# One hybrid decoder layer: a scan constant in PSUM, carries read from the scan buffers, fused operations, and GLA queries decayed in one pass

## The chip, the cores and the metric

The kernel runs on one core of a Trainium2 chip. The metric is the device time of one execution in microseconds (us). The five engines named below are TensorE (PE in the profile; PEld are its weight loads), VectorE (DVE), ScalarE (ACT), GpSimd (POOL) and SyncE (SP, which here only issues transfers). They run side by side, each in its own fixed order, and wait for each other through semaphores. SBUF is the on-chip memory of 128 partitions; PSUM is the smaller memory of eight banks into which TensorE writes.

## The reference

One decoder layer on 2048 positions of width 1024, in float32: three token mixers on the same normalised input, one output projection with residual, and a gated FFN with residual.

```python
h = rms_norm(x, norm_mix_g)
gq, gk, gv, g_lr, g_gate, sq, sk, sv, hq, hf, hi, h_gate = split(h @ w_in)
# A) GLA, 4 heads of 48 / 96, and C) HGRN2, 4 heads of 128 / 64: gated linear recurrences
#    S_t = diag(exp(log_f_t)) S_{t-1} + k_t^T v_t ;  o_t = q_t S_t
o_a = rms_norm(gla(gq, gk, gv, log_alpha)) * silu(g_gate)
o_c = rms_norm(gla(hq, 1 - f, hi, log_f)) * silu(h_gate)
# B) stick-breaking attention, 6 heads of 64, strictly causal:
z = q_b @ k_b.T * 64 ** -0.5
A[t, s] = sigmoid(z[t, s]) * prod_{s < j < t} (1 - sigmoid(z[t, j]))
o_b = rms_norm(A @ v)
x = x + concat(o_a, o_b, o_c) @ w_out
gate, up = split(rms_norm(x) @ w_ffn_up)
return x + (silu(gate) * up) @ w_ffn_down          # d_ff = 2816
```

## The kernel before, in words

Matrix products run in TensorE's fp32r format with each operand split into a high part and the rest (`split`, `conv_w`: ACT makes the high part, DVE or POOL the rest), three matmuls per product: high·high, high·low, low·high. The two FFN products are also split into seven block products of half size, numbered 1 to 7, whose operands are sums and differences of blocks (`sub`, `add`).

The work goes through stages. *Input projections* come first. Then the *mixers* run together. Attention is cut into units of one head, one group of 512 queries and one block of 512 keys, and each unit into four steps of 128 queries. `z_step` computes z on TensorE, two sigmoids on ACT (`kp` for 1 − sigmoid, `w` for sigmoid), a running product of `kp` from the last key to the first on DVE (L993, `tensor_tensor_scan`, whose second operand is not used: `op1` is bypass), and the product `w` · `pr` on POOL, or on DVE for some steps (L997). The last value of the running product is the carry into the next key block: POOL copies it into a column of its own (`ca`, L996). `t_step` transposes `w`, five steps behind, and `a_step` multiplies it with the values, seven steps behind. The two recurrences work on chunks of 128 positions (`hg_chunk`, `gla_chunk`) in levels of doubling block size (`decay_levels`): at each level queries and keys are multiplied by decays (DVE L1071 and L1112, POOL L1117 and L1106), the decays by each other (POOL L1121), TensorE forms the scores (`sch`, `scg`), and a copy by mask (DVE L1075) takes them out of PSUM. GLA's two heads share a partition range, so that its queries lie in two copies that see the same decays. The recurrences' score tiles take turns in a ring of three PSUM banks (`c_pss`).

TensorE's order in the mixers is fixed by the program's order (`Chain`); the other engines are ordered by a scheduler that follows a simulated timeline. Attention's end overlaps the *output projection* (`Out`): `load` fetches a tile of 128 positions and normalises its heads (14 squares on ACT with their sums, DVE multiplies, POOL gates), `turn` transposes it, three matmuls per block multiply it, `norm` and `left` prepare the FFN's input, which `left_sums` stores in DRAM as `xs_s`.

*FFN up* goes over two halves of the positions and 22 blocks of columns, the seven products in the order 1, 5, 6, 2, 3, 7, 4; `left_in` loads and converts the left operands (`ah`, `al`). *FFN down* runs the seven products in the order 1, 2, 5, 6, 3, 7, 4, each over 11 steps k with eight PSUM banks. `left_dn` and `right_dn` load (`ar`, `br`, chains `xa`, `xb`), combine and convert each step's operands (`dah`, `dal`, `dbh`, `dbl`); `flush_dn` adds a finished product to the accumulators `acc`, which start from the residual, and stores finished quarters to `out`. All these transfers are issued by SP, one after the other. Every tile takes its buffer from a pool with a number of buffers (`bufs`), and a new tile waits until the last use of the one before in its buffer.

Of the kernel before, what the change touches and what calls it, by code (L numbers as in the profile page):

```python
# [19 lines left out]
P = 128  # L20
# [42 lines left out]
def hybrid_block(ctx: ExitStack, tc: tile.TileContext, x, norm_mix_g, w_in, gla_w_decay,  # L63
# [740 lines left out]
    class Out:  # L804
        def open(self):
# [5 lines left out]
            self.pt = open_pool(self.st, "d_pt", 1, PSUM, side="right")  # L811

        def load(self, t):
# [15 lines left out]
            dve.tensor_scalar(ms[:, 4:14], ms[:, 4:14], 1.0 / SD, EPS, op0=ALU.mult,  # L829
                              op1=ALU.add)  # L830
            rs = rsqrt_newton(self.sm, ms, 14, "rm")
            for a, b, w, i, j in segs:
                mv = m[:, a:b].rearrange("p (h d) -> p h d", d=w)
# [3 lines left out]
            pool.tensor_tensor(m[:, 768:], m[:, 768:], gt[:, 384:], op=ALU.mult)  # L837
            mv = m[:, 384:768].rearrange("p (h d) -> p h d", d=SD)
            pool.tensor_tensor(mv, mv, gs64.unsqueeze(1).to_broadcast([P, SH, SD]), op=ALU.mult)
# [4 lines left out]
        def turn(self, prep, hf):  # L844
            t, m, _, mh, ml = prep
            pt = self.pt.tile([P, 4, P], F32, tag="pt", name=f"mt{t}_{hf}")
# [15 lines left out]
        def left(self, t, xt, kh):  # L862

            pt = self.pt.tile([P, KH, P], F32, tag="pt", name=f"xt{t}_{kh}")
# [61 lines left out]
    with ExitStack() as ph:  # L926
# [11 lines left out]
        ps_s = open_pool(prc, "c_pss", 3, PSUM)  # L938
# [20 lines left out]
        def z_step(u, b):  # L959
            h, g, c = u.h, u.g, u.c  # L960
            if b == 0:
                if u.diag:
                    u.q = sio.tile([P, 2, 512], F32, tag="sq", name=f"sq{h}_{g}", bufs=3)
                    for s in range(2):
# [3 lines left out]
                    u.carry = [sbk.tile([P, 1], F32, tag=f"ca{i}", name=f"ca{h}_{g}_{i}", bufs=4)  # L968
                               for i in range(4)]
                else:  # L970
                    p = units[u.i - 2]
                    u.q, u.carry = p.q, p.carry
# [12 lines left out]
            if u.diag:  # L985
# [3 lines left out]
            pr = sbk.tile([P, 513], F32, tag="pr", name=f"pr{h}_{g}_{c}_{b}")  # L989
            act.activation(kp[:, :n], z, AF.Sigmoid, scale=-1.0)  # L990
            act.activation(w, z, AF.Sigmoid)  # L991
            kr = kp[:, n::-1] if n < 512 else kp[:, ::-1]
# [4 lines left out]
            (dve if (b in DVE_B0 if g == 0 else b == DVE_B) else pool).tensor_tensor(w, w, pr[:, 1:n + 1], op=ALU.mult)  # L997
            u.ws.append(w)

        def t_step(u, s):  # L1000
# [5 lines left out]
            wh = sbw.tile([P, 512], F32, tag="wth", name="wth" + nm, bufs=8)[:, t0:]  # L1006
# [43 lines left out]
        def decay_levels(nm, nq, nk, q, k, f, st, score, block, hold, eng, qeng):  # L1050
# [9 lines left out]
            def tv(ap, s, h, rep):  # L1060

                m = ap.shape[2] // 2
                v = ap.rearrange("p n (b s) -> p n b s", s=2)[:, :, :, s]
                return v.unsqueeze(3).to_broadcast([P, nk, m, h])
# [529 lines left out]
```

## Time and profile before

| | |
|---|---|
| median of 3 runs (lowest, highest) | 3147.08 us (3138.09, 3147.41) |
| profiled execution | 3147.62 us, its span 3145.8 us |
| TensorE busy, weight loads | 2831.5 us (90%), 2309.9 us |
| VectorE, ScalarE, GpSimd busy | 2116.2 (67%), 1344.4 (43%), 1639.2 us (52%) |
| transfers | 389.82 MB, mean 124 GB/s |

The page divides the span into 40 slices. Each digit is the busy share of a slice in tenths, and PEclk is the clock granted to TensorE, in tenths of full speed:

```profile
PE   5898999997888889878888799999999997899998
DVE  8886665886888888988866455555755553267443
PEclk9999999998889998989988899999999998999999
```

### The profile page before, as it was taken

Reading aid. Unit: us, or ns where it says so; the run is one execution under the profiler, and the core shown is the slowest. Engines: PE = TensorE matmul, PEld = TensorE weight load, DVE = VectorE, ACT = ScalarE, POOL = GpSimd, SP = SyncE. Lnnn points to the kernel's source line nnn. Section 1 sums busy time; section 2 is a strip of 40 time slices with the busy share of each in tenths; the row PEclk is TensorE's granted clock in tenths of the full one; section 3 lists DMA queues with packets and bytes.
Section 4 is the critical chain, followed back from the end, with each engine's and each line's share of the span. In section 5 each row is a group of like instructions: output and inputs, shape, how many; then the busy total and the mean of one; then the engine's idle time right before and its main releaser. Section 6 shows DMA issues by size and latency. Waiting matters only on the chain. (4 is left out here: it accounts for less than half of the span.)

```text
span 3145.8 us, 43879 instructions
## 1 busy us (share of the span) xinstructions
PE 2831.5 (90%) x14882; PEld 2309.9 (73%) x14882; DVE 2116.2 (67%) x3508; ACT 1344.4 (43%) x2834; POOL 1639.2 (52%) x1640
## 2 busy tenths in 40 slices
PE   5898999997888889878888799999999997899998
PEld 5897878996666666655666588888788885677776
DVE  8886665886888888988866455555755553267443
ACT  5554534453555555566644333333433332323222
POOL 5342554344787887854633244444544442257635
PEclk9999999998889998989988899999999998999999
DMA  3534432536533333123354332222422225564173
GB/s 116 159 108 134 139 127 97 136 94 166 153 104 107 98 100 93 58 94 108 130 173 161 134 114 85 87 87 84 142 87 81 81 81 216 212 234 144 64 241 131
DMA packets 346095, 389.82 MB, mean 124 GB/s; under 512 B 59152, under 2 KB 258064, under 8 KB 344080
## 3 DMA queue, kind: packets, MB, share of 16 engines
q1 hardware_dynamic: 341776, 381.77, 38.4%
q0 software_dynamic: 4096, 5.25, 0.5%
q8 instruction: 119, 1.95, 0.3%
q14 instruction: 104, 0.85, 0.1%
HBM read 278.93 MB, written 108.00 MB: 123 GB/s over the span
## 5 line engine op out<-in xcount | busy, mean ns | idle before, releaser
L1390 PE MATMUL gu<-ah,uh 128*128 128x512 f32 x1232 | 481.3, 391 | 10.1 <-ACT ah L248 10.1
L1391 PE MATMUL gu<-al,uh 128*128 128x512 f32 x1232 | 481.8, 391 | 6.0 <-DVE al L249 5.9
L1392 PE MATMUL gu<-ah,ul 128*128 128x512 f32 x1232 | 481.0, 390 | 0.0
L249 POOL TENSOR_TENSOR ul<-bs,uh 128x512 fp32r<-128x512 f32 x176 | 241.6, 1374 | 243.2 <-ACT uh L248 243.2
L249 POOL TENSOR_TENSOR ul<-us,uh 128x512 fp32r<-128x512 f32 x132 | 176.6, 1339 | 203.6 <-ACT uh L248 203.6
L1390 PEld LDWEIGHTS gu<-ah,uh 128*128 128x128 f32 x1232 | 232.3, 189 | 60.3 <-ACT ah L248 12.0
L1391 PEld LDWEIGHTS gu<-al,uh 128*128 128x128 f32 x1232 | 232.5, 189 | 56.9 <-DVE al L249 8.7
L1552 PE MATMUL dn<-dbh,dah 128*128 128x512 f32 x616 | 224.6, 402 | 48.4 <-ACT dbh L248 41.8
L1392 PEld LDWEIGHTS gu<-ah,ul 128*128 128x128 f32 x1232 | 232.3, 189 | 48.1
L245 DVE TENSOR_TENSOR h<-h,gu 128x512 f32<-128x512 f32 x176 | 120.9, 687 | 205.3 <-PE gu L1392 123.5
L1553 PE MATMUL dn<-dbl,dah 128*128 128x512 f32 x616 | 243.9, 396 | 12.7 <-POOL dbl L249 12.6
L1554 PE MATMUL dn<-dbh,dal 128*128 128x512 f32 x616 | 242.4, 395 | 3.1 <-DVE dal L249 3.0
L248 ACT ACTIVATE uh<-bs 128x512 fp32r<-128x512 f32 x176 | 110.9, 632 | 299.8 <-PE gu L1391 299.6
L993 DVE TENSOR_TENSOR_SCAN pr<-kp,ca 128x513 f32<-128x513 f32 x144 | 213.2, 1484 | 22.0 <-ACT kp L990 17.7
L997 POOL TENSOR_TENSOR w<-w,pr 128x512 f32<-128x512 f32 (+1 forms) x174 | 191.8, 1102 | 46.0 <-DVE pr L993 26.0
L990 ACT ACTIVATE kp<-z 128x512 f32<-128x512 f32 (+1 forms) x240 | 128.0, 533 | 183.4 <-PE z L104 168.7
L104 PE MATMUL z<-sk,sq 128*128 128x512 f32 (+1 forms) x480 | 170.7, 440 | 14.5 <-ACT w L991 8.1
L107 PE MATMUL wt<-ident,w 128*128 128x128 f32 x816 | 147.9, 294 | 39.2 <-POOL w L997 34.3
L1552 PEld LDWEIGHTS dn<-dbh,dah 128*128 128x128 f32 x616 | 118.4, 194 | 80.5 <-ACT dbh L248 49.3
L249 DVE TENSOR_TENSOR dal<-ar,dah 128x1024 fp32r<-128x1024 f32 x44 | 65.0, 1485 | 163.1 <-ACT dah L248 163.0
L248 ACT ACTIVATE uh<-us 128x512 fp32r<-128x512 f32 x132 | 83.1, 631 | 193.0 <-PE gu L1391 130.6
L104 PEld LDWEIGHTS z<-sk,sq 128*128 128x128 f32 x480 | 80.7, 208 | 104.7 <-issue 37.9
(385 smaller groups left out, 7845.1 us busy)
## 6 DMA issues: line engine op xcount, KB each, us to landing
us<-in_w_ffn_up SPq DMA_DIRECT2D x88, 512.0 KB, 3.8
ar<-hs_s SPq DMA_DIRECT2D x88, 512.0 KB, 4.0
hs_s<-h SPq DMA_DIRECT2D x44, 512.0 KB, 2.6
br<-in_w_ffn_down SPq DMA_DIRECT2D x88, 256.0 KB, 3.2
sk<-sk_s SPq DMA_DIRECT2D x60, 256.0 KB, 2.9
st<-xs_s SPq DMA_DIRECT2D x14, 1024.0 KB, 5.2
xt<-in_x SPq DMA_DIRECT2D x24, 512.0 KB, 4.8
sq<-sq_s SPq DMA_DIRECT2D x48, 256.0 KB, 4.8
```

The source lines that it names most:

```text
L104: self._add(nc.tensor.matmul(*a, **k))
L107: self._add(nc.tensor.transpose(*a, **k))
L248: act.activation(wh, st, AF.Copy)
L249: eng.tensor_tensor(wl, st, wh.bitcast(F32), op=ALU.subtract)
L993: dve.tensor_tensor_scan(pr[:, n::-1], kr, kr, 1.0 if u.diag else u.carry[b], op0=ALU.mult, op1=ALU.bypass)
L997: (dve if (b in DVE_B0 if g == 0 else b == DVE_B) else pool).tensor_tensor(w, w, pr[:, 1:n + 1], op=ALU.mult)
L1390: pe.matmul(pv, bh[:, k, :], ah[:, :, k, :], start=(k == 0), stop=False)
L1391: pe.matmul(pv, bh[:, k, :], al[:, :, k, :], start=False, stop=False)
L1392: pe.matmul(pv, bl[:, k, :], ah[:, :, k, :], start=False, stop=(k == KH - 1))
L1552: pe.matmul(pss[i], ah[:, ts_], bh, start=(k == 0), stop=False)
L1553: pe.matmul(pss[i], ah[:, ts_], bl, start=False, stop=False)
L1554: pe.matmul(pss[i], al[:, ts_], bh, start=False, stop=(k == NK - 1))
```

## The change

*Mixers.* The scan's unused operand becomes a column of ones in a PSUM bank of its own (`c_ps1`), for as long as the recurrences run; the score ring `c_pss` has two banks instead of three. The 47 scans that come after the recurrences keep the old operand. Two scan buffers with shifted views (`at`) hold the carries, so that the next scan reads the last column of an earlier one and the copies to `ca` go. GLA's decays `ga` are loaded twice, and a level multiplies both copies of the queries by one instruction. The states' decay and sum become one fused DVE instruction for each head or pair (`scalar_tensor_tensor`), 60 + 30 of them, in place of 30 products on POOL and 30 sums on DVE.

*Output projection.* A tile's 14 squares on ACT become one, with three sums on DVE; normalising and gating become 14 fused DVE instructions in place of three DVE and three POOL products. Three more PSUM banks (`d_px`) hold transposes once the mixers are through.

*FFN up.* The first `ah`, `al` buffers are taken in the reverse order of the products, which changes whose space the first one reuses.

*FFN down.* The order becomes 1, 5, 6, 2, 3, 7, 4; loads keep the program's order; `br` has three buffers; products 5 and 7 are added to both accumulators from PSUM on DVE (before, ACT copied them and POOL added the copy); half of product 6's adds are put off, two for each step of the next product.

```diff
+            sq = self.wk.tile([P, D], F32, tag="sq", name=f"msq{t}", bufs=1)
+            act.activation(sq, m, AF.Square)
             for a, b, w, i, j in segs:
-                for h in range(j - i):
-                    sj = self.sm.tile([P, GDV], BF16, tag="sj", name=f"sj{t}_{i}_{h}", bufs=1)
-                    act.activation(sj[:, :w], m[:, a + h * w:a + (h + 1) * w], AF.Square,
-                                   accum_out=ms[:, i + h:i + h + 1])
+                dve.tensor_reduce(ms[:, i:j], sq[:, a:b].rearrange("p (h d) -> p h d", d=w),
+                                  axis=AX.X, op=ALU.add)
...
-                dve.tensor_tensor(mv, mv, rs[:, i:j].unsqueeze(2).to_broadcast([P, j - i, w]),
-                                  op=ALU.mult)
-            pool.tensor_tensor(m[:, 0:384], m[:, 0:384], gt[:, 0:384], op=ALU.mult)
...
+                    dve.scalar_tensor_tensor(m[:, cs], m[:, cs], rs[:, n:n + 1], g_,
+                                             op0=ALU.mult, op1=ALU.mult)
...
-        ps_s = open_pool(prc, "c_pss", 3, PSUM)
+        ps_s = open_pool(prc, "c_pss", 2, PSUM)
+        ps_1 = open_pool(prc, "c_ps1", 1, PSUM)
+        ones = [ps_1.tile([P, 512], F32, name="one")[:, 0:1]]
+        dve.memset(ones[0], 1.0)
...
+        prs = [sbk.tile([P, 513 + 16], F32, name=f"pr{i}", bufs=1) for i in range(2)]
...
-            pr = sbk.tile([P, 513], F32, tag="pr", name=f"pr{h}_{g}_{c}_{b}")
+            at = 4 * (g - c) + 2 * u.j + b // 2
+            pr = prs[b % 2][:, at:at + 513]
...
-            dve.tensor_tensor_scan(pr[:, n::-1], kr, kr, 1.0 if u.diag else u.carry[b],
-                                   op0=ALU.mult, op1=ALU.bypass)
-            if c > 0:
-                pool.tensor_copy(u.carry[b], pr[:, 0:1])
...
+            dve.tensor_tensor_scan(pr[:, n::-1], kr,
+                                   ones[0].to_broadcast([P, n + 1]) if ones else kr,
+                                   u.carry[b], op0=ALU.mult, op1=ALU.bypass)
+            u.last.append(pr[:, 0:1])
...
             def q_mul(h, tcur):
-                lo = tv(tcur, 0, h, r)
-                qq = q.rearrange("p (n r) t -> p n r t", r=r)
-                for j in range(r):
-                    qu = up(qq[:, :, j, :], h, 1)
-                    qeng.tensor_tensor(qu, qu, lo, op=ALU.mult)
+                qu = up(q, h, 1)
+                qeng.tensor_tensor(qu, qu, tv(tcur, 0, h), op=ALU.mult)
...
-            pool.tensor_tensor(s_new, s_old, dec.to_broadcast([P, HH, HDV]), op=ALU.mult)
-            dve.tensor_tensor(s_new, s_new, pu, op=ALU.add)
+            for i in range(HH):
+                dve.scalar_tensor_tensor(s_new[:, i, :], s_old[:, i, :], dec[:, i, :], pu[:, i, :],
+                                         op0=ALU.mult, op1=ALU.add)
...
+    out_.ptx = open_pool(ptx, "d_px", 3, PSUM)
...
+    ops = {m: tuple(hp.tile([P, 4, KH, P], F32R, tag=f"{x}{m}", name=f"{x}{m}_0")
+                    for x in ("ah", "al")) for m in ORDER[::-1]}
...
+    bop = open_pool(pd, "g_bo", 3, side="right")
...
     def load_a(t_, k, j, kh):
-        dma.dma_start(t_, hs_s[kh * NK + k][j].rearrange("p i j t -> p (i j t)"))
+        tc.keep_in_program_order(
+            dma.dma_start(t_, hs_s[kh * NK + k][j].rearrange("p i j t -> p (i j t)")))
...
-            tmp = rop.tile([P, 512], F32, tag="tmp", name=f"tmp{m}_{i}")
-            act.activation(tmp, ps, AF.Copy)
             add(c, c, ps)
-            add(c22, c22, tmp, pool)
+            add(c22, c22, ps)
...
-            add(c12, c12, u, pool)
             add(c21, c21, u)
-            add(c22, c22, u, pool)
+            later.append(lambda: add(c12, c12, u, pool))
+            later.append(lambda: add(c22, c22, u, pool))
...
-    for m in (1, 2, 5, 6, 3, 7, 4):
+    for m in (1, 5, 6, 2, 3, 7, 4):
```

On GpSimd in the middle of the mixers there stood, before (the names' digits are head, query group, key block and step; `hk` and `gk` are recurrence keys, `th` and `tg` decays):

```order
L996 COPY ca2_2_2_11582<-pr2_2_2_2_11644 128x1
L997 TENSOR_TENSOR w2_2_2_2_11643<-w2_2_2_2_11643,pr2_2_2_2_11644 128x384
L1117 TENSOR_TENSOR gk_7_11253<-gk_7_11253,tg7_16_11657 128x4x32
L1121 TENSOR_TENSOR th9_32_12535<-th9_16_12478 128x8
L996 COPY ca2_2_3_11583<-pr2_2_2_3_11681 128x1
L1106 TENSOR_TENSOR hk_8_11707<-hk_8_11707,hf_8_11708 128x256
L1121 TENSOR_TENSOR tg9_16_12566<-tg9_8_12494 128x8
L1121 TENSOR_TENSOR th9_64_12602<-th9_32_12535 128x4
L996 COPY ca3_2_0_11726<-pr3_2_2_0_11737 128x1
L997 TENSOR_TENSOR w2_2_2_3_11680<-w2_2_2_3_11680,pr2_2_2_3_11681 128x512
```

and now, with the same products:

```order
L1008 TENSOR_TENSOR w2_2_2_2_11411<-w2_2_2_2_11411,pr0_8059 128x384
L1127 TENSOR_TENSOR gk_7_11041<-gk_7_11041,tg7_16_11422 128x4x32
L1131 TENSOR_TENSOR th9_32_12253<-th9_16_12198 128x8
L1118 TENSOR_TENSOR hk_8_11469<-hk_8_11469,hf_8_11470 128x256
L1131 TENSOR_TENSOR tg9_16_12277<-tg9_8_12213 128x16
L1008 TENSOR_TENSOR w2_2_2_3_11445<-w2_2_2_3_11445,pr1_8060 128x512
```

The copies to `ca` are gone, and with them three waits for scans; of the other products here only `th9_64` stands elsewhere.

On SP at the start of FFN down there stood, before (`ar1_4` is the left block of product 1, step 4; `br1_0` the right one of step 0; `xa`, `xb` are blocks for product 5):

```order
L1454 DMA ar1_4_00_25805<-hs_s4_0_255 128x1024
L1454 DMA xa9_26887<-hs_s9_1_266 128x1024
L1454 DMA xa10_26929<-hs_s10_1_268 128x1024
L1454 DMA ar1_5_00_25841<-hs_s5_0_257 128x1024
L1458 DMA br1_0_00_25635<-in_w_ffn_down 128x512
L1458 DMA br1_1_00_25671<-in_w_ffn_down 128x512
L1458 DMA xb0_26518<-in_w_ffn_down 128x512
L1458 DMA xb1_26560<-in_w_ffn_down 128x512
```

and now:

```order
L1477 DMA ar1_0_00_24842<-hs_s0_0_247 128x1024
L1481 DMA br1_0_00_24848<-in_w_ffn_down 128x512
L1477 DMA ar1_1_00_24878<-hs_s1_0_249 128x1024
L1481 DMA br1_1_00_24884<-in_w_ffn_down 128x512
L1437 DMA hs_s21_1_290<-h1_21_24664 128x1024
L1477 DMA ar1_2_00_24914<-hs_s2_0_251 128x1024
L1481 DMA br1_2_00_24920<-in_w_ffn_down 128x512
L1581 DMA acc0_24950<-x2_s0_217 128x1024
```

The first steps' `ar` and `br` are issued in turn, ahead of the loads for product 5; the accumulator loads follow the third pair.

On SP at the border from product 7 to product 4 there stood, before:

```order
L1458 DMA br7_8_11_28245<-in_w_ffn_down 128x512
L1458 DMA br7_8_01_28247<-in_w_ffn_down 128x512
L1454 DMA ar4_0_11_28410<-hs_s11_1_270 128x1024
L1454 DMA ar4_1_11_28447<-hs_s12_1_272 128x1024
L1458 DMA br7_9_11_28287<-in_w_ffn_down 128x512
L1458 DMA br7_9_01_28289<-in_w_ffn_down 128x512
L1454 DMA ar4_2_11_28484<-hs_s13_1_274 128x1024
L1458 DMA br7_10_11_28329<-in_w_ffn_down 128x512
L1458 DMA br7_10_01_28331<-in_w_ffn_down 128x512
L1454 DMA ar4_3_11_28521<-hs_s14_1_276 128x1024
L1458 DMA br4_0_10_28416<-in_w_ffn_down 128x512
L1458 DMA br4_1_10_28453<-in_w_ffn_down 128x512
```

and now:

```order
L1481 DMA br7_10_01_27528<-in_w_ffn_down 128x512
L1542 DMA out_0<-acc8_24966 128x512
L1542 DMA out_0<-acc9_24968 128x512
L1542 DMA out_0<-acc10_24970 128x512
L1542 DMA out_0<-acc11_24972 128x512
L1542 DMA out_0<-acc12_24974 128x512
L1542 DMA out_0<-acc13_24976 128x512
L1542 DMA out_0<-acc14_24978 128x512
L1542 DMA out_0<-acc15_24980 128x512
L1477 DMA ar4_0_11_27591<-hs_s11_1_270 128x1024
L1481 DMA br4_0_10_27597<-in_w_ffn_down 128x512
```

The eight stores of product 7's accumulators are issued ahead of product 4's first loads; before, product 4's loads were ahead of those of product 7's last steps.

## Rows read from the trace of the kernel before

**Rows 1.** Four stretches: span, busy by engine (instructions), PEclk, DMA share, GB/s

```profile
755.00:1420.00 665.00, 571.83 (x3998) 431.60 (x3999) 560.40 (x895) 368.46 (x927) 514.03 (x757) 0.90 0.38 108
1420.00:1575.00 155.00, 134.61 (x668) 92.48 (x667) 132.31 (x246) 101.78 (x317) 84.49 (x87) 0.96 0.37 119
1575.00:1784.00 209.00, 165.66 (x725) 127.15 (x724) 120.16 (x338) 79.69 (x290) 62.95 (x54) 0.87 0.47 153
2639.00:3146.00 507.00, 438.27 (x1849) 352.52 (x1848) 240.49 (x187) 136.10 (x179) 251.07 (x153) 0.94 0.53 186
```

**Rows 2.** DVE's groups by form, 755 to 1420 us: busy, mean ns, idle before

```profile
L993 DVE TENSOR_TENSOR_SCAN pr<-kp,ca 128x513 f32<-128x513 f32 x110 | 161.9, 1474 | 16.0 <-ACT kp L990 13.0 <-POOL w L997 1.7 <-ACT sj L826 1.1
L1071 DVE TENSOR_TENSOR qx_g<-qx_g,tg 128x128 f32<-128x128 f32 x192 | 89.2, 503 | 17.2 <-PE scg L104 17.2
L1071 DVE TENSOR_TENSOR hq<-hq,th 128x256 f32<-128x256 f32 x96 | 59.3, 618 | 1.2 <-PE sch L104 1.0
L1075 DVE COPY_PREDICATED st_g<-masks,scg 128x256 f32<-128x256 int8 x96 | 55.6, 579 | 11.2 <-PE scg L104 10.9
```

**Rows 3.** Instructions of tile kp: ns min/median/max

```profile
L993 DVE TENSOR_TENSOR_SCAN pr<-kp,ca x144: 1247/1286/2356, 856.2 to 1569.7; 128x513 f32<-128x513 f32 x144
```

**Rows 4.** The timeline near 917 us, POOL and DVE: start, us

```profile
916.77 1.09 POOL L997 TENSOR_TENSOR w<-w,pr 128x512 f32<-128x512 f32 x1
917.30 1.65 DVE L993 TENSOR_TENSOR_SCAN pr<-kp,ca 128x513 f32<-128x513 f32 x1 [0.42 <-ACT kp L990]
```

**Rows 5.** The timeline near 1101 us, the same two engines

```profile
1101.28 0.73 DVE L1075 COPY_PREDICATED st_g<-masks,scg 128x256 f32<-128x256 int8 x1
1101.36 1.09 POOL L997 TENSOR_TENSOR w<-w,pr 128x512 f32<-128x512 f32 x1
```

**Rows 6.** The waits between 755 and 1420 us: us, times, longest

```profile
PE wt L107 <- POOL w L997: 23.3, 21, 3.8
PE sch L104 <- POOL hk L1117: 11.5, 10, 5.1
DVE qx_g L1071 <- PE scg L104: 17.2, 13, 5.3
```

**Rows 7.** POOL's copies of carries, 755 to 1420 us

```profile
L996 POOL COPY ca<-pr 128x1 f32<-128x1 f32 x118 | 35.9, 306 | 48.7 <-DVE pr L993 43.9 <-PE scg L104 1.8 <-PE wt L107 1.4
```

**Rows 8.** ACT's and DVE's groups by form, 1575 to 1784 us

```profile
L826 ACT ACTIVATE sj<-m 128x64 bf16<-128x64 f32 x78 | 19.9, 255 | 2.2
L826 ACT ACTIVATION_READ_ACCUMULATOR sj<-m 128x1 f32 x106 | 19.8, 187 | 0.0
L857 ACT ACTIVATE mh<-xt 128x1024 fp32r<-128x1024 f32 x11 | 11.6, 1053 | 7.7 <-DVE xt L907 7.7
L84 DVE SCALAR_TENSOR_TENSOR rmy<-rma,rmy 128x14 f32<-128x14 f32 x24 | 6.7, 280 | 0.5
```

**Rows 9.** Instructions of tile m: ns min/median/max

```profile
L834 DVE TENSOR_TENSOR m<-m,rmy x48: 413/558/1316, 1412.9 to 1723.0; 128x384 f32<-128x384 f32 x32, 128x256 f32<-128x256 f32 x16
```

**Rows 10.** The timeline at the start of FFN up

```profile
1784.79 0.79 PE L1390 MATMUL gu<-ah,uh 128*128 128x512 f32 x1 [7.53 <-ACT ah L248]
```

**Rows 11.** The timeline at the start of FFN down, SP and PE

```profile
2665.94 15.97 SPq L1558 DMA_DIRECT2D acc<-x_s  x16
2662.54 2.08 PE L1552 MATMUL dn<-dbh,dah 128*128 128x512 f32 x4 [23.53 <-ACT dbh L248]
2693.27 2.08 PE L1552 MATMUL dn<-dbh,dah 128*128 128x512 f32 x4 [12.75 <-ACT dbh L248]
```

**Rows 12.** PE's waits between 2639 and 3146 us

```profile
PE dn L1552 <- ACT dbh L248: 41.8, 8, 23.5
PE dn L1553 <- POOL dbl L249: 12.6, 6, 6.0
```

**Rows 13.** DVE's adds of products, 2639 to 3146 us

```profile
L245 DVE TENSOR_TENSOR acc<-acc,dn 128x512 f32<-128x512 f32 x48 | 31.4, 681 | 28.1 <-ACT tmp L1528 18.6 <-PE dn L1554 9.5
```

**Rows 14.** The page's DMA issues: KB, us to landing

```profile
ar<-hs_s SPq DMA_DIRECT2D x88, 512.0 KB, 4.0
```

More of the change, by code (lines that the diff above doesn't have):

```diff
@@ L811, in open, with pt_tile @@
             self.pt = open_pool(self.st, "d_pt", 1, PSUM, side="right")
+            self.ptx = None
+        def pt_tile(self, name):
+            return (self.ptx or self.pt).tile([P, KH, P], F32, tag="pt", name=name)
         def load(self, t):
@@ L845, in turn @@
             t, m, _, mh, ml = prep
[L846 removed]
+            pt = self.pt_tile(f"mt{t}_{hf}")
             for j in range(4):
@@ L967, in z_step @@
                                       .rearrange("j p t -> p j t"))
-                    u.carry = [sbk.tile([P, 1], F32, tag=f"ca{i}", name=f"ca{h}_{g}_{i}", bufs=4)
-                               for i in range(4)]
+                    u.carry = [1.0] * 4
                 else:
                     p = units[u.i - 2]
-                    u.q, u.carry = p.q, p.carry
+                    u.q, u.carry = p.q, p.last
+                u.last = []
                 k = sio.tile([P, 512], F32, tag="sk", name=f"sk{h}_{g}_{c}")
@@ L1109, in decay_levels @@
                 if h == 1:
-                    qq = q.rearrange("p (n r) t -> p n r t", r=r)
-                    for j in range(r):
-                        qeng.tensor_tensor(qq[:, :, j, :], qq[:, :, j, :], f, op=ALU.mult)
+                    qeng.tensor_tensor(q, q, f, op=ALU.mult)
                     q_mul(1, tcur)
@@ L1205, in gla_chunk @@
             dma.dma_start(k, gk_s[g][:, :, o:o + P])
-            dma.dma_start(f, ga_s[g][:, :, o:o + P])
+            for s in range(2):
+                dma.dma_start(f[:, :, s, :], ga_s[g][:, :, o:o + P])
             dma.dma_start(v, gv_s[c].rearrange("p (h d) -> p h d", d=GDV))
@@ L1219, in block @@
                               stop=True)
-            dec = yield from decay_levels(f"g{c}", GH, 2, qv, k, f, st, score, block, None,
+            dec = yield from decay_levels(f"g{c}", GH, 2, qv, k,
+                                          f.rearrange("p n r t -> p (n r) t"), st, score, block, None,
                                           pool, dve)
@@ L1246, in gla_chunk @@
             s_new = rec.tile([P, 2, GDV], F32, tag="s_g", name=f"s_g_{c}", bufs=2)
-            pool.tensor_tensor(s_new, s_old, dec.to_broadcast([P, 2, GDV]), op=ALU.mult)
-            dve.tensor_tensor(s_new, s_new, pu, op=ALU.add)
+            for i in range(2):
+                dve.scalar_tensor_tensor(s_new[:, i, :], s_old[:, i, :], dec[:, 2 * i, :], pu[:, i, :],
+                                         op0=ALU.mult, op1=ALU.add)
             state["g"] = s_new
@@ L1300, in hybrid_block @@
                 prc.close()
+                ones.clear()
                 out_.open()
@@ L1371, in left_in @@
         st = stp.tile([P, 4, KH, P], F32, tag="st", name=f"st{ip}_{m}")
-        hi, lo = (hp.tile([P, 4, KH, P], F32R, tag=f"{x}{m}", name=f"{x}{m}_{ip}")
-                  for x in ("ah", "al"))
+        hi, lo = (ops[m] if ip == 0 else
+                  (hp.tile([P, 4, KH, P], F32R, tag=f"{x}{m}", name=f"{x}{m}_{ip}")
+                   for x in ("ah", "al")))
         dma.dma_start(st, xs_s[ip][m])
@@ L1513, in right_dn, with done @@
         return hi, lo
-    held = {}
+    held, later = {}, []
+    def done(t, hf):
+        cs = slice(hf * 512, hf * 512 + 512)
+        dma.dma_start(out[t * P:(t + 1) * P, cs], acc[t][:, cs])
     def flush_dn(m, i, ps):
@@ L1559, in hybrid_block @@
                     acc.append(a)
+            for fn in later[:2]:
+                fn()
+            del later[:2]
         for i in range(8):
             flush_dn(m, i, pss[i])
+    for fn in later:
+        fn()
     pd.close()
```

65 lines of the change are left out of this document (35 added, 30 removed).

## The prediction

> **What bounds the kernel now.** I read the busy line first, then the slices, and then cut the span where the busy pattern changes. FFN up, from 1784 to 2639 us, is filled by TensorE; apart from its first matmul the change leaves it alone, as it does everything before 755 us. Four stretches are left [rows 1]. From 755 to 1420 us the attention and the two recurrences run together: TensorE is busy for 572 of 665 us and VectorE for 560, or 84%. No engine is full there, so I read the waits: TensorE waits for GpSimd's products (23.3 and 11.5 us), VectorE for TensorE's scores (17.2 us) [rows 6]. It is a ring in which VectorE has least room after TensorE. From 1420 to 1575 us the end of attention overlaps the output projection, VectorE at 85%. From 1575 to 1784 us the projection runs alone and no engine is full: VectorE 57%, TensorE 79%, so that chains of short steps set the pace. From 2639 us, FFN down, TensorE would be full but for waits: 41.8 us for converted weights, 12.6 us for their low halves [rows 12].
>
> **What VectorE and GpSimd do to each other.** The 144 full scans take 1247 ns at the least and 1286 in the middle, but 1474 on average in the first stretch [rows 2, 3]: a tail, not a constant. One row of it: GpSimd's multiply began at 916.77 and ended at 917.86; the scan began at 917.30 and took 1.65 us, 0.40 over the minimum [rows 4]. The scan reads `kp` twice, both times from SBUF. A copy by mask, which takes one operand from PSUM, began at 1101.28, 0.08 us ahead of the same multiply, and that took its 1.09 us [rows 5]. So the engines hold each other up where both of a VectorE instruction's tensors are in SBUF, and the constant in PSUM should end that for scans.
>
> **The change part by part.** The profiled execution took 3147.6 us, 0.5 over the median of the runs, so sums against it stand for both.
>
> *First stretch (755 to 1420).* The scans' tail is (1474 − 1247) ns × 110 = 25 us [rows 2, 3]; it goes entirely (−25) or not at all (0); by the pair of rows 4 and 5 I take −25. The GLA queries: 192 × 503 ns = 89 us become 96 of double width, priced as the HGRN2 product of that shape, 618 ns, 59 us: −30 [rows 2]. The two forms that halve in number and double in width I put at nothing, since width costs what the count gives back. The states: 90 fused instructions in place of 30 adds, 60 more; at the 280 ns of a fused instruction of 14 columns [rows 8] that is +17. VectorE: 560 − 38 = 522 us. GpSimd loses 118 carry copies (36 us, and 44 us in which it stood waiting for the scan with later products queued behind [rows 7]), and all state products; wider decay products give a few us back. Nothing is late in their place, since the next scan reads the carry from the buffer. If the ring keeps VectorE's share, 522/0.843 = 619: −46. The ends are 0 (TensorE's own order holds) and −93 (TensorE without a gap). I take **−46**, near the middle, because both engines that TensorE waits for are relieved.
>
> *Overlap (1420 to 1575).* Here I expect a cost. Per tile of the output projection ACT's 14 squares of 0.255 + 0.187 us = 6.2 us become one of 1.05 us [rows 8], GpSimd's three products go, and VectorE exchanges three multiplies for three sums (passes over the same columns, 0.41 to 1.3 us each [rows 9], put equal) and gains 14 fused instructions: 14 × 0.280 = 3.9 us. The squares' 106 reads after 1575 us are about eight tiles of the sixteen [rows 8]; one loads before 1420, so some seven here: +27 on 132 us of 155. The carry copies and GpSimd's products that lengthened VectorE's work go too, but the last scans keep their SBUF operand. 159 us cannot be hidden in 155; some relief from GpSimd comes off. I take **+5**, from −15 to +20. [...]
>
> *Projection alone (1575 to 1784).* Eight tiles add 31 us to VectorE's 120: 151 us, which at the share of the first stretch needs 179 of the 209, −30. The path of a tile from load to transposition shortens by 5 us on ACT and 3 on GpSimd against 4 on VectorE, and three more transposition buffers let TensorE run ahead. But this stretch is a chain, and VectorE's part of it grows; I take two thirds, **−20**; ends +5 and −43 (TensorE's 166 us).
>
> *Start of FFN up.* The first conversion no longer waits for a buffer that the last stores hold. TensorE waited 7.53 us there [rows 10]; what is late next is the conversion, about one us: **−6**, ends 0 and −7.5.
>
> *FFN down.* Before, SP issued eleven right-hand and left-hand blocks for later products ahead of the weights: TensorE waited 23.53 us, and again 12.75 us for weights behind the 16 accumulator loads, whose issue alone took 15.97 us [rows 11]. After, the first two blocks of both operands are issued first, but the accumulator loads still stand ahead of the fourth block. 36 us become some 3 + 12: −21. Against it: each product's output stores now stand on SP ahead of the next product's first loads, and each store waits for the flush add. At the borders after products 2, 3 and 7 a load can only be issued after the adds: 0.68 us [rows 13] + 4.0 us to land [rows 14] + about 2 us of subtraction and conversion ≈ 7 us each; after product 7, 16 adds (10.9 us) make it 12. That is 26 us, against 18 us of such waits before (54.4 in rows 12 less 36.3): +8. The sum is **−12**, from −35 (all borders hidden) to +15.
>
> Together: −46 + 5 − 20 − 6 − 12 = −79 us, 3069 us.
>
> **Rivals.**
> 1. *Banks.* Recurrence scores lose one of three PSUM banks. TensorE's order is fixed, so a score product that finds both banks full stops everything behind it. With 192 masked copies of 0.58 us [rows 2], a full copy waited for each time costs 111 us: 3069 + 111 = 3180. Slower begins where more than 0.41 us is lost per copy. For it: copies queue behind scans. Against it: VectorE now waits for scores, 17.2 us in one row [rows 6], rather than the reverse.
> 2. *Relief without speed.* The ring is set by latencies of TensorE and ACT, or the scan gains nothing from the PSUM constant. Then the first stretch gives 0 to −15 and the rest −33: 3100 to 3115. For it: TensorE's 572 of 665. [...]
> 3. *TensorE's floor.* GpSimd's freedom counts more than VectorE's. First stretch −80, projection −40, overlap −10, FFN down −20, start −6: 3147 − 156 = 2991.
> 4. *VectorE full after 1420.* Drawn out by GpSimd as that scan was, the 14 small instructions cost 0.4 us each: +45 us over eight tiles, and seven tiles bring +39 to the overlap. VectorE at 165 of 209 with its part of the chain 5.6 us longer leaves the projection no gain, and the overlap loses 20: 3069 + 20 + 15 = 3104.
>
> **How the numbers follow.** Forecast (3040 to 3095) 0.45; relief without speed or VectorE full, 0.26 together, of which 0.04 ends within the bound and 0.01 above; TensorE's floor, 0.18; banks, 0.11, of which 0.02 is still a gain and 0.02 none either way. A measurement tells 0.3%, 9.4 us, from no change. Faster: 0.45 + 0.21 + 0.18 + 0.02 = 0.86. Same: 0.04 + 0.02 = 0.06. Slower: 0.01 + 0.07 = 0.08. The range runs from 2990 (rival 3) to 3125 (beyond rivals 2 and 4); outside lie most of the banks and what exceeds rival 3.
>
> **What would show it.** After: scans with the constant near 1.25 us on average, and GpSimd's multiplies no longer stretched under them; no copy of carries; VectorE's share of the first stretch still about 84% with the stretch some 45 us shorter (a higher TensorE share at lower VectorE share means rival 3; new waits of TensorE for masked copies mean rival 1). In the projection VectorE near 13 us per tile. One first gap of a few us in FFN down, one of about 12 us behind the accumulator loads, and new ones of 7 to 12 us at the last three borders. Wrong would be the whole if the first stretch kept its 665 us.

## The result, and the profile after

The changed kernel takes 3110.88 us (median of 4 runs, 3108.39 to 3119.01) where the kernel before takes 3145.18 us; the ratio is 0.9901, interval 0.9883 to 0.9920. Run again later beside other versions it gave 0.9877 (0.9859 to 0.9896). It is faster by about 34 us. The forecast was faster, by 79 us: the side was right and the range held the time, but the size was more than double of what came.

To see where the time went I cut both profiled executions at the first or last matmul of a kind. The first stretch runs from the first `z` product to the last product of a recurrence, the overlap to the last `av`, the projection to the last `xt` transposition, FFN up (its start included) to the last `gu`, then the gap before the first `dn`, and the rest. Each border is the start of the matmul named.

| us | before | after | difference | forecast |
|---|---|---|---|---|
| first stretch | 638.8 | 617.5 | −21.3 | −46 |
| overlap | 197.4 | 198.6 | +1.2 | +5 |
| projection | 185.9 | 175.9 | −10.0 | −20 |
| start of FFN up, FFN up | 861.8 | 862.2 | +0.4 | −6 |
| gap before FFN down | 23.9 | 3.3 | −20.6 | −12 with the next row |
| FFN down | 483.2 | 499.1 | +15.9 | |
| span | 3145.8 | 3111.6 | −34.2 | −79 |

The stretches as engines saw them, for comparison with [rows 1], with the same columns and the borders moved with the work:

```profile
755.00:1398.00 643.00, 566.34 (x4000) 424.73 (x4000) 518.61 (x860) 360.36 (x853) 392.55 (x606) 0.92 0.41 115
1398.00:1555.00 157.00, 135.19 (x670) 92.33 (x669) 138.98 (x337) 85.13 (x164) 49.51 (x40) 0.97 0.37 117
1555.00:1748.00 193.00, 157.68 (x720) 124.33 (x718) 132.58 (x439) 49.48 (x85) 34.86 (x27) 0.90 0.49 159
2609.00:3111.00 502.00, 439.60 (x1851) 357.89 (x1849) 252.46 (x203) 127.79 (x163) 238.31 (x137) 0.93 0.53 187
```

The figures behind the span are TensorE, its weight loads, VectorE, ScalarE and GpSimd, then the granted clock. In the first stretch VectorE lost 42 us of work, 4 more than the forecast, and GpSimd 121, and the stretch lost only 22. Busy time fell and the span did not follow it, so a new wait is the first suspect. The scans are not it. These are their rows after (ns, min/median/max; for [rows 3]), with the constant and, once the recurrences are over, without it:

```profile
L1001 DVE TENSOR_TENSOR_SCAN pr<-kp,pr,one x105: 1243/1271/1285, 845.9 to 1374.0; 128x513 f32<-128x513 f32 x105
L1001 DVE TENSOR_TENSOR_SCAN pr<-kp,pr x39: 1253/1279/2099, 1376.3 to 1545.2; 128x513 f32<-128x513 f32 x39
```

With the constant in PSUM the longest of 105 scans is 42 ns over the shortest; the 39 with both tensors in SBUF still have their tail. Counted over the traces: before, the 28 of the 144 scans of [rows 3] that no GpSimd instruction overlapped took 1255 to 1287 ns, and the other 116 up to 2356; after, 92 of the 105 with the constant were overlapped and none took more than 1285. What TensorE waited for in the first stretch (for [rows 6]):

```profile
PE ho L104 <- DVE st_h L1087: 7.6, 3, 2.6
PE z L104 <- DMA sk<-sk_s: 5.8, 1, 5.8
PE sch L104 <- DVE s_h L1203: 5.4, 5, 1.6
PE sch L104 <- DVE hq L1083: 5.4, 5, 1.4
PE ho L104 <- DVE st_g L1087: 4.9, 2, 2.9
PE scg L104 <- DVE qx_g L1083: 4.7, 3, 2.1
PE wt L107 <- POOL w L1008: 4.6, 6, 2.3
PE sch L104 <- DVE st_h L1087: 3.7, 5, 1.7
PE hpk L107 <- DVE st_g L1087: 3.6, 2, 2.0
PE hpk L107 <- DVE st_h L1087: 3.5, 4, 2.0
```

The waits for GpSimd are nearly gone. In their place stand waits for masked copies (`st_g`, `st_h`) and state sums (`s_h`). `hpk` is the telling name: it transposes keys and reads neither mask copy, so what it waits for is a PSUM bank that the copy has yet to empty. (`ho` reads `st_h`, so not every wait in these rows is for a bank; the experiments tell how much of them is.) VectorE's other groups (for [rows 2]; busy, mean ns):

```profile
L1083 DVE TENSOR_TENSOR hq<-hq,th 128x256 f32<-128x256 f32 x96 | 72.2, 752 | 0.1
L1083 DVE TENSOR_TENSOR qx_g<-qx_g,tg 128x256 f32<-128x256 f32 x96 | 61.6, 642 | 20.5 <-PE scg L104 20.5
```

The queries cost 61.6 us, forecast 59, but the HGRN2 product beside them grew from 618 to 752 ns; why is not shown.

The longer of TensorE's waits in FFN down after (start, duration; in brackets the idle time before and what ended it), for [rows 11]:

```profile
2612.49 2.07 PE L1575 MATMUL dn<-dbh,dah 128*128 128x512 f32 x4 [2.91 <-ACT dbh L248]
2642.42 1.65 PE L1575 MATMUL dn<-dbh,dah 128*128 128x512 f32 x3 [11.71 <-ACT dbh L248]
2834.79 0.80 PE L1576 MATMUL dn<-dbl,dah 128*128 128x512 f32 x1 [6.03 <-POOL dbl L249]
2896.39 1.22 PE L1575 MATMUL dn<-dbh,dah 128*128 128x512 f32 x2 [8.37 <-ACT dah L248]
2969.67 1.65 PE L1575 MATMUL dn<-dbh,dah 128*128 128x512 f32 x3 [10.25 <-ACT dbh L248]
3045.09 1.65 PE L1575 MATMUL dn<-dbh,dah 128*128 128x512 f32 x3 [12.82 <-ACT dbh L248]
```

The first two are as forecast (3 and 12 us), the last three a little longer (7, 7 and 12). The one at 2834.79 was not forecast.

### The profile page after: what moved, and what is told of

Read it like the earlier page. It is cut to its first block, busy times and chain, and to the rows that moved or that the text cites. A ratio compares the mean times of both kernels' runs of the same rounds, so it can differ in the third digit from the quotient of the medians.

```text
span 3111.6 us, 43456 instructions
## 1 busy us (share of the span) xinstructions
PE 2821.7 (91%) x14882; PEld 2305.4 (74%) x14882; DVE 2111.8 (68%) x3681; ACT 1281.7 (41%) x2386; POOL 1445.6 (46%) x1402
## 4 chain that ended last, share of the span: by engine, by line
PE 59%; DVE 14%; issue 4%; DMA 4%; POOL 2%; ACT 2%; SPq 0%; DVEq 0%; POOLq 0%; ACTq 0%
PE gu L1410 9%; PE gu L1411 9%; PE gu L1409 9%; PE dn L1575 4%; PE dn L1576 4%; PE dn L1577 4%; PE z L104 3%; DVE pr L1001 2%; PE av L104 2%; PE wt L107 2%; PE sch L104 2%; PE scg L104 1%; DVE m L840 1%; PE ho L104 1%; DMA m<-mx_s 1%
## 5 line engine op out<-in xcount | busy, mean ns | idle before, releaser
L1575 PE MATMUL dn<-dbh,dah 128*128 128x512 f32 x616 | 235.5, 408 | 50.0 <-ACT dbh L248 37.7
L1001 DVE TENSOR_TENSOR_SCAN pr<-kp,pr,one 128x513 f32<-128x513 f32 x105 | 133.6, 1272 | 23.1 <-ACT kp L997 21.8
```

Source lines behind the costliest of these rows:

```text
L1001: dve.tensor_tensor_scan(pr[:, n::-1], kr, ones[0].to_broadcast([P, n + 1]) if ones else kr, u.carry[b], op0=ALU.mult, op1=ALU.bypass)
L1575: pe.matmul(pss[i], ah[:, ts_], bh, start=(k == 0), stop=False)
```

## The experiments

Ratios are to the kernel before, run beside them on the same chip; the groups a to d were on three chips. Stretches and waits come from one profile of each version: in nine profiles of kernels that share the changed kernel's first stretch it took 614 to 620 us.

**The bank and the operand.** The theory: the third score bank, given for the constant, cost what the first stretch was to gain. The rival: latencies of TensorE and ScalarE set the ring, and no relief can show. Four kernels cross the two.

```diff
 a1: changed kernel, scan operand kp, three score banks
-        ps_s = open_pool(prc, "c_pss", 2, PSUM)
+        ps_s = open_pool(prc, "c_pss", 3, PSUM)
...
-        ones = [ps_1.tile([P, 512], F32, name="one")[:, 0:1]]
+        ones = []
 a2: the same with two score banks
 a3: kernel before
-        ps_s = open_pool(prc, "c_pss", 3, PSUM)
+        ps_s = open_pool(prc, "c_pss", 2, PSUM)
 a4: changed kernel with the constant
-        ps_s = open_pool(prc, "c_pss", 2, PSUM)
+        ps_s = open_pool(prc, "c_pss", 3, PSUM)
-        ps_w = open_pool(ph, "f_pw", 2, PSUM)
+        ps_w = open_pool(ph, "f_pw", 1, PSUM)
```

> The changed kernel, but the scan's unused operand is kp again (SBUF) and the score ring has its third PSUM bank back. Bank theory (the lost third bank ate the relief: about 30 us of new TensorE waits for VectorE's masked copies and state sums in the first stretch): these waits fall to under 8 us, the scans' tail of some 25 us of VectorE time comes back; the stretch is 5 us shorter to 8 us longer than in the changed kernel, the time 3100 to 3118. Latency theory (TensorE's and ScalarE's latencies set the ring, whatever the banks): nothing gained by the bank, 3111 to 3125, with the waits for copies only moved to other names.

> The changed kernel, but the scan's unused operand is kp again (SBUF), with two score banks; the bank of ones is simply not used. Bank theory: it has the short ring and the scans' tail, 12 to 30 us above the changed kernel, 3123 to 3141, and at least 15 us above the version with three banks. Latency theory: within 8 us of both, 3108 to 3120.

> The kernel before with two score banks in place of three and nothing else changed. Bank theory: 15 to 40 us above the kernel before, 3160 to 3185, by TensorE waits for masked copies and sums. Latency theory: within 5 us of it, 3140 to 3150.

> The changed kernel with three score banks and the constant in PSUM; the bank is taken from the ring of transposed weights (one instead of two). Bank theory: waits for masked copies under 8 us (30 us less), but each transposition now waits for the copy of the one before it (ScalarE, 0.6 us, 240 of them): 3085 to 3130, and the two effects show in separate waits. Latency theory: only the loss shows, 3125 to 3170.

In the table the waits are sums over TensorE's rows in the view of waits, from 755 us to the end of the first stretch, by releaser: GpSimd, or VectorE's masked copies and state sums. VectorE and GpSimd are their busy times in it.

| | operand, banks | ratio | stretch us | waits: GpSimd | copies, sums | VectorE | GpSimd |
|---|---|---|---|---|---|---|---|
| before | kp, 3 | 1 | 638.8 | 48.9 | 7.8 | 541 | 501 |
| a3 | kp, 2 | 1.0009 (0.9993 to 1.0024) | 652.1 | 35.5 | 41.4 | 541 | 500 |
| a1 | kp, 3 | 0.9948 (0.9931 to 0.9966) | 629.2 | 45.3 | 9.1 | 541 | 497 |
| a2 | kp, 2 | 0.9973 (0.9961 to 0.9985) | 647.0 | 29.9 | 41.8 | 534 | 490 |
| after | one, 2 | 0.9901 (0.9883 to 0.9920) | 617.5 | 9.6 | 38.5 | 496 | 386 |
| a4 | one, 3 | 0.9789 (0.9765 to 0.9814) | 594.0 | 11.1 | 6.7 | 495 | 386 |

The columns separate: the operand decides both engines' busy time and most of the waits for GpSimd, the banks alone decide the waits for copies and sums. These are 31 us more in the changed kernel than before, and with the third bank back 6.7 us are left. a4's longest rows, but for a load, name none of them:

```profile
PE sch L104 <- DVE hq L1083: 13.0, 10, 2.4
PE wt L107 <- ACT wth L1018: 10.7, 7, 2.6
PE scg L104 <- DVE qx_g L1083: 6.9, 5, 3.6
PE wt L107 <- POOL w L1008: 4.0, 7, 1.6
```

The single bank for transposed weights is paid in the second row, 10.7 us, and a4 is still 0.9 to 1.1% faster than the changed kernel (0.9789 against 0.9877 and 0.9901). So the rival theory falls.

The waits are not the whole of it. The first stretch of the changed kernel and of a4 (columns as in [rows 1]):

```profile
755.00:1373.00 618.00, 552.58 (x3940) 417.20 (x3941) 495.84 (x784) 346.06 (x828) 385.94 (x601) 0.92 0.41 113
755.00:1350.00 595.00, 532.96 (x3935) 404.22 (x3936) 494.55 (x784) 344.83 (x827) 385.76 (x601) 0.95 0.42 118
```

Of the 23 us that a4 is shorter, TensorE's idle time gives only some 4, since other waits came in place of those for copies (13.0 us for `hq` instead of 5.4, and the second row). The other 19 or so are its busy time: the same products ran faster, at a granted clock of 0.95 instead of 0.92. That the bank brought this about is what the totals say; why the clock rose here is open, for in the two pairs with `kp` it was no higher with three banks than with two (0.91 and 0.91, 0.90 and 0.91).

My expectations held for a4 (3085.63 us, at the edge of 3085 to 3130), not for the three others. a1 came out at 3132.87 us, above its 3100 to 3118, and a2 at 3143.28: the operand is worth more than the scans' 25 us (1.6% between a1 and a4, though a4 even pays for the transpositions). GpSimd is freed as well, but here too half of the 35 us by which a4's stretch is shorter is TensorE's busy time (552 against 533 us).

And a3 was not slower in all, which is what the rival expected: its first stretch is 13 us longer, but the total shows +0.09% with an interval that holds zero. TensorE's waits for GpSimd fell by 13 us as those for copies rose by 34, and in the profile the overlap was 6 us shorter and the first `z` product came 4 us earlier. By the totals the third bank is worth nothing that shows in the kernel before (0.09%), 0.25% with `kp` in the changed one (a1 against a2; the intervals touch) and about 1% with the constant: it counts most where TensorE no longer waits for GpSimd. The a1 row tells one thing more: with the operand left in SBUF, all other edits of the stretch (queries in one pass, carries, fused states) give 10 us, and neither engine's busy time falls by more than 4 us.

**The projection.** Two edits meet there. b1 (and d3, the same) puts the old normalising back; b4 (and d2, the same) takes the extra transposition banks out.

```diff
 b1, d3
-            act.activation(sq, m, AF.Square)
+                    act.activation(sj[:, :w], m[:, a + h * w:a + (h + 1) * w], AF.Square,
+                                   accum_out=ms[:, i + h:i + h + 1])
...
 b4, d2
-    out_.ptx = open_pool(ptx, "d_px", 3, PSUM)
```

> The changed kernel with the old normalising of the output projection's tiles (14 squares on ScalarE, three products each on VectorE and GpSimd); the three extra transposition banks stay. If the shorter path of a tile made the projection faster (the prediction's step): the stretch from the last attention product to the last transposition, 176 us in the changed kernel, is 180 to 190 us, the time 5 to 15 us above the changed kernel. If the extra banks did it: 174 to 178 us, the time within 4 us.

> The changed kernel without the three extra PSUM banks for transpositions at the end of the output projection. With the old normalising the projection alone takes 164 us, with the new one 176 us, before 186 us. If the banks gave about 22 us and the new normalising took 12 back: the projection takes 185 to 200 us here, the time 10 to 22 us above the changed kernel. If the new normalising's shorter path gave the gain and the banks little: 174 to 180 us, the time within 4 us.

The ratios were 0.9839 (0.9817 to 0.9860) for b1 and 0.9905 (0.9889 to 0.9921) for b4, against 0.9901 for the changed kernel, each against the kernel before of its own group: by them the old normalising gains 20 us and the banks nothing, which the profiles contradict. So both ran again on one chip with the changed kernel.

> The changed kernel itself, on the same chip as the three below, as their common base: 0.990 of the kernel before, 0.986 to 0.993.

> The version without the extra transposition banks beside the changed kernel on one chip. Its projection alone was 16.5 us longer in one profile, while the two ratios hardly differed. If the banks are worth their 16 us: 10 to 18 us above the changed kernel of this call. If the following stages give it back: within 4 us.

> The changed kernel with the old normalising, beside the changed kernel on one chip. Profiles showed 12 us less in the projection alone and 6 us more in the overlap. By these: 4 to 10 us under the changed kernel of this call; by the ratios of the earlier calls (0.9839 and 0.9901): 15 to 24 us under it.

| | ratio | overlap us | projection us |
|---|---|---|---|
| d1, changed kernel | 0.9877 (0.9859 to 0.9896) | 200.0 | 175.8 |
| d2, no extra banks | 0.9925 (0.9908 to 0.9943) | 198.4 | 191.2 |
| d3, old normalising | 0.9860 (0.9843 to 0.9877) | 201.6 | 168.6 |

The extra banks are worth 0.48%, 15 us, and the projection shows the same 15. The old normalising takes 7 us off the projection (12 in b1) and costs 2 to 6 in the overlap; its total is no different from the changed kernel's, as the intervals overlap. b1's 20 us were not repeated. The reason is in the projection's busy times (columns as in [rows 1]), first of the changed kernel, then of d3:

```profile
1571.00:1747.00 176.00, 141.27 (x646) 113.63 (x642) 126.71 (x416) 44.83 (x77) 34.13 (x26) 0.90 0.51 167
```

```profile
1575.00:1744.00 169.00, 142.06 (x641) 114.04 (x640) 110.43 (x315) 71.61 (x266) 55.97 (x49) 0.90 0.53 171
```

With the new normalising VectorE does 16 us more and ScalarE 27 us less. TensorE's waits for the two halves of the transposed tile, `mh` from ScalarE and `ml` from VectorE, are 15.0 and 13.2 us with it and 9.0 and 6.2 without; that VectorE's part ahead of them sets the pace is my reading, not shown apart. Its fused instructions, from 1392 to 1747 us:

```profile
L840 DVE SCALAR_TENSOR_TENSOR m<-m,rmy,gs 128x64 f32<-128x64 f32 x96 | 29.0, 369 | 0.0
L840 DVE SCALAR_TENSOR_TENSOR m<-m,rmy,gt 128x96 f32<-128x96 f32 x64 | 20.1, 372 | 0.5
L840 DVE SCALAR_TENSOR_TENSOR m<-m,rmy,gt 128x64 f32<-128x64 f32 x64 | 17.1, 326 | 0.0
```

They are 66.2 us of busy time for 224, 0.30 us each (instructions that follow each other overlap, so the means are higher), close to the 0.280 that I had taken. The median is 280 ns for the first row's and 305 for the other two together; the means are raised by some that ran beside GpSimd and took up to 1403.

**The start of FFN up.** b2 takes the first buffers in the old order again.

```diff
-    ops = {m: tuple(hp.tile([P, 4, KH, P], F32R, tag=f"{x}{m}", name=f"{x}{m}_0")
-                    for x in ("ah", "al")) for m in ORDER[::-1]}
```

> The changed kernel without the reversed taking of FFN up's first buffers. Prediction's step (6 us saved at the start): the time is 5 to 7 us above the changed kernel. Rival (the early start only meets the pace at which the other left operands are loaded and converted, so it is given back): from the last transposition to the last product of FFN up stays at 862 us within 2 us, the time within 3 us, with the gap of 6 to 8 us back in front of the first product.

It gave 0.9887 (0.9871 to 0.9903), no different from the changed kernel. From the last transposition to the last product of FFN up it takes 862.3 us against 862.2, so that the rival is right in the time. Its side remark, that the gap in front of the first product would come back, was wrong: in that version the first product came 1.6 us after the last transposition too, so this edit was not what closed the gap. Every version of the changed kernel has it closed, those without the extra banks or with the old normalising too, and a3 has it open; which edit closed it stays unknown. What takes the early start back is seen in the rows of the changed kernel:

```profile
1748.60 8.03 DVE L249 TENSOR_TENSOR al<-st,ah 128x512 fp32r<-128x512 f32 x6 [3.27 <-ACT ah L248]
1754.38 0.32 SPq L1393 DMA_DIRECT2D st<-xs_s  x1
1761.29 0.50 PE L1409 MATMUL gu<-ah,uh 128*128 128x512 f32 x1 [2.96 <-ACT ah L248]
```

and of the kernel before:

```profile
1784.77 4.87 DVE L249 TENSOR_TENSOR al<-st,ah 128x512 fp32r<-128x512 f32 x6 [10.54 <-ACT ah L248]
1787.30 18.95 SPq L1374 DMA_DIRECT2D st<-xs_s  x5
```

The first low halves are formed in 8.0 us instead of 4.9, while GpSimd forms the sums of the last tiles (that these slow them is not shown apart), and the load of the next operand, which takes over their buffer, is issued 5.8 us after the start instead of 2.5.

**FFN down.** b3 makes three edits, d4 only the first.

```diff
 b3 and d4: stores are put off
-        dma.dma_start(out[t * P:(t + 1) * P, cs], acc[t][:, cs])
+        stores.append((out[t * P:(t + 1) * P, cs], acc[t][:, cs]))
...
+            if k > 0:
+                store(2)
 b3 alone: two accumulators loaded per step, put-off adds pinned
-            if m == 1 and k == 2:
-                for t in range(NT):
+            if m == 1 and k >= 2:
+                for t in range(2 * k - 4, min(2 * k - 2, NT)):
...
+        tc.keep_in_program_order(pool.tensor_tensor(c, c, u, op=ALU.add))
```

> The changed kernel with three edits in FFN down: output stores issued two at a time after the next product's second and later loads, accumulator loads two per step instead of 16 in a row, and GpSimd's put-off adds pinned to their steps. If stores ahead of loads, the 16 accumulator loads and the bunched adds make TensorE's waits there (8.5 + 10.4 + 13.0, 11.9, and 8.9 us): all fall to under 3 us but for the adds at the last border, and FFN down is 28 to 45 us shorter, 3068 to 3083. If the loads' own pace (buffers, transfer bandwidth) is behind them: 5 to 18 us shorter, with the waits at the same places under other names.

> The changed kernel with one of the three FFN down edits: output stores issued after the next product's second and later loads. If stores ahead of loads make the waits at the last three borders (8.5, 10.4, 13.0 us): these fall to under 2 us each, the gaps behind the 16 accumulator loads (11.9) and the bunched adds (8.9) stay, and with the half clock behind each wait the time is 28 to 40 us under the changed kernel of this call. If the loads' pace is behind them: under 12 us.

b3 gave 3046.08 us, 0.9674 (0.9659 to 0.9688), and d4 3075.07 us, 0.9764 (0.9750 to 0.9779), beside 0.9877 for the changed kernel on d4's chip. FFN down took 499.1 us in the changed kernel, 460.3 in d4, 435.2 in b3. TensorE's waits there in d4:

```profile
PE dn L1580 <- ACT dbh L248: 16.0, 3, 12.2
PE dn L1581 <- POOL dbl L249: 6.6, 3, 6.0
PE dn L1580 <- DVE acc L245: 5.5, 3, 3.3
```

and in b3:

```profile
PE dn L1583 <- DVE acc L245: 3.5, 2, 3.1
PE dn L1583 <- ACT dbh L248: 3.4, 2, 2.9
PE dn L1584 <- POOL dbl L249: 0.7, 2, 0.4
PE dn L1585 <- DVE dal L249: 0.6, 1, 0.6
```

The stores ahead of loads are the cause at the three borders: their waits (8.37, 10.25 and 12.82 us) are gone in d4. The other two, 12.2 us behind the 16 accumulator loads and 6.0 us behind GpSimd's adds, go with the two further edits of b3, each in its own place. The adds had been put off in the program, two per step, but stood bunched in GpSimd's order all the same, as the changed kernel's row shows, eight ahead of one low half:

```profile
2817.78 14.75 POOL L245 TENSOR_TENSOR acc<-acc,u 128x512 f32<-128x512 f32 x8
2832.49 2.24 POOL L249 TENSOR_TENSOR dbl<-br,dbh 128x512 fp32r<-128x512 f32 x1
```

b3 gained more than I expected (3068 to 3083); d4 met its range. The waits of TensorE fell by 50 us (58.6 summed over the changed kernel's rows of that view to 8.2), FFN down by 64. The rest is TensorE's busy time, 439 us in the changed kernel and 426 in b3 for the same 1848 products, at a granted clock of 0.93 and 0.99. In the changed kernel the clock was 1.00 before the wait of 11.71 us, 0.50 in the 3.6 us behind it, and 0.92 in the next 4.

**A version that beats both.** c1 joins a4 and b3; c2 adds the old normalising for tiles 8 to 15, c3 for all.

```diff
 c2
+            if t < 8:
+                sq = self.wk.tile([P, D], F32, tag="sq", name=f"msq{t}", bufs=1)
+                act.activation(sq, m, AF.Square)
...
+            else:
+                for a, b, w, i, j in segs:
```

> The changed kernel with three score banks (the transposed weights' ring has one) and the three edits in FFN down. The places lie apart, so the gains should add: 35 us for the banks and what the FFN down edits give alone (28 to 45 us): 3030 to 3050. Rival: FFN down's edits give only 5 to 18 us: 3058 to 3073.

> The combined version (three score banks, reordered FFN down), with the new normalising for tiles 0 to 7, which load while attention still runs, and the old one for tiles 8 to 15. If the 14 fused instructions cost where VectorE is in the chain, and spare ScalarE where attention runs: the projection alone 162 to 170 us in place of 179, the overlap 199 within 3 us, the time 9 to 17 us under the combined version's 3022 (3005 to 3013). If the gain of the old normalising was noise between runs: within 4 us of 3022.

> The combined version with the old normalising for all tiles. Chain theory: the projection alone 162 to 168 us, the overlap 3 to 8 us longer than the combined version's 199, the time 5 to 14 us under 3022 and not under the half-and-half version. Noise theory: within 4 us of 3022.

c1 took 3022.51 us, 0.9601 (0.9587 to 0.9616), a shorter time than I expected; yet taking both gains from the changed kernel's mean ratio, 0.989 − 0.010 − 0.0215 = 0.9575, some 8 us more should have come. In the profiles 5 us of a4's gain lay in FFN down, which a4 doesn't touch, and c1's projection took 3 us more than the changed kernel's. c2 took 3015.90 us, 0.9577 (0.9559 to 0.9594), c3 3012.72 us, 0.9572 (0.9545 to 0.9600). Their projections took 163.6 and 164.6 us against 178.9, as expected, and the overlap did not suffer (197.6 and 198.0 against 199.2), where I had expected c3's to be 3 to 8 us longer; so keeping the new normalising for half the tiles has no point. c2's time just missed its 3005 to 3013. The intervals of c2 and c3 touch that of c1, so in the total their gain over c1 is likely rather than shown. c2 and c3 are not told apart, and c3 is simpler: 4.3% faster than the kernel before, about 3% faster than the changed one.

## Why the prediction was wrong in size

- *First stretch, −46 against −21.* The step that failed is "If the ring keeps VectorE's share", with the loss of the bank put at nothing. VectorE's own sum was about right: 45 us less against 38. But the share did not stay: it fell from 541/639 = 0.85 to 496/618 = 0.80, while TensorE's waits for copies and sums, most of them for banks, rose from 7.8 to 38.5 us. I had this as the first rival, with that very sign, but priced it only as a reason for a slower kernel (0.41 us per copy) and held it unlikely (0.11) on a row of before in which VectorE waited for scores. The waits are 31 us over 192 copies, 0.16 us each: too little to turn the sign, enough to take half of the forecast. A rival with a price should have stood in the sum with a part of it. With the bank back (a4) the share is 0.83 and the stretch lost 45 us, almost the forecast, though a wait for another bank had been added. That 45 meets 46 is in part luck: most of the last 23 us came as faster products, and the sum had no term for the clock. VectorE's sum was lucky too: the 88 scans without a carry, left out, fell by 14 us, the HGRN2 product grew by 13, and the states cost 9 instead of 17.
- *The scan.* Right, and worth more than taken. The pair of rows 4 and 5 was thin evidence, since the multiply took its 1.09 us in both; the count above carries it. The sign for GpSimd's multiplies did not come in the form given: `w` · `pr` took 1185 ns on average before and 1222 after; with the operand back in SBUF (a1) it took 1352, against 1210 in a4. The shortest scan is 1243 ns with the constant and 1253 without. VectorE and GpSimd were busy 47 us (541.4 to 494.6) and 112 us (497.5 to 385.8) less with the constant in a4 than in a1, and 38 and 104 us less in the changed kernel than in a2, which differ in the operand alone.
- *Queries and states.* The queries came out right (61.6 us for 59; 192 × 503 ns would be 97, the 89 is the row's busy time), their worth did not: without the operand all edits of the stretch move it 10 us, and VectorE is as busy as before (541 us).
- *Overlap, +5 against +1, and projection, −20 against −10.* VectorE's work was put too high in both: it came to 139 us, not 159, and to 133, not 151, so the cost of the first hardly came. In the second the two parts pull against each other: the extra banks −15, the new normalising +7 to +12. The failed step is the shorter path of a tile, which I counted as a gain: 27 us less on ScalarE gained nothing, and 16 more on VectorE cost 7 to 12. The 280 ns that I took for a fused instruction is a mean with a tail: of the 48 of `rmy` in the trace of before, 24 of them in rows 8, the median is 174 ns, and the five over 176 ns, 815 to 1246, all ran beside GpSimd. The 0.4 us of rival 4 was an estimate of mine, these 280 ns drawn out as the scan of rows 4 was; measured, the 224 new ones took 0.30 us each.
- *Start of FFN up, −6 against 0.* The gap closed, by 6.3 us, though not by the edit that I credited (b2), and was given back within 30 us: what was late next was not one conversion, as I wrote, but the load behind it.
- *FFN down, −12 against −5* (the terms, −21 and +8, make −13). The gap before it and the one behind the accumulator loads were right (3 and 12 us). The borders cost 31 us instead of 26, since a load waits for all eight stores and with them for all eight adds (at the first of them the eight adds took 5.45 us from 2883.30, the stores' issue 5.09 us from 2884.01, and the load was issued at 2889.20). The put-off adds, 6.0 us in one row, I had held to be spread.

## What to carry to other kernels

When a change takes a buffer from a ring, price the wait for it and put a part of that price into the sum, even where the wait is too small to turn the sign; look afterwards for consumers that wait for an engine whose result they don't read. Where an engine's busy time falls without the span following, the waits by releaser, before and after, name in one table what is waited for instead; beside them belong TensorE's own busy time and granted clock, for a change that takes waits away can also bring faster products (b3: 439 to 426 us, at a clock of 0.93 and 0.99). And a queue that issues both stores and loads should not have a store that waits for arithmetic ahead of the loads of the next stage (here TensorE waited 8.37, 10.25 and 12.82 us behind such stores).

## What the runs showed of the hardware

GpSimd gained more than VectorE from VectorE's operand moved to PSUM: 112 us of busy time against 47 (a1 and a4), 104 against 38 (a2 and the changed kernel). Its own instructions did not change for it: the 96 products of HGRN2's keys took 954 ns on average in a1 and 706 in a4. These are the rows before and after:

```profile
L1117 POOL TENSOR_TENSOR hk<-hk,th 128x256 f32<-128x256 f32 x96 | 92.3, 962 | 16.4 <-PE sch L104 14.9 <-PE o L107 1.1
L1127 POOL TENSOR_TENSOR hk<-hk,th 128x256 f32<-128x256 f32 x96 | 67.0, 698 | 46.6 <-PE sch L104 46.0 <-DVE qx_g L1083 0.3
```

Scans with two SBUF operands kept a spread to the end of attention (1253 to 2099 ns), those with one in PSUM had almost none (1243 to 1285).
